# Layer 0's attention: the modulation rows summed by pairs of K-tiles over all 1024 columns, and turned into columns once per part

## The chip, the cores and the metric

The kernel runs on one core of one Trainium2 chip. The metric is the device time of one execution in microseconds (us); a lower time is better. The engines are PE (TensorE: matmuls and transposes; its weight loads are PEld), DVE (VectorE), ACT (ScalarE), POOL (GpSimd) and SP (SyncE, which issues nearly all DMA transfers). Each engine works through its own queue in order, and the engines wait for one another by semaphores.

## The reference, cut to what matters

The reference is a block of two transformer layers over 512 latent and 256 context tokens of width 1024. Each layer needs six modulation vectors of 1024 numbers (shift, scale and gate, for attention and for the FFN), each of them for two streams, latent and context:

```
s_c = silu(c);  s_cc = silu(c_ctx)
mx = s_c  @ mod_w[l] + mod_b[l]        # 1024 x 6144, latent stream
mc = s_cc @ mod_w[l] + mod_b[l]        # the same weights, context stream
shx1, scx1, gx1, shx2, scx2, gx2 = split(mx, 6)
hx = rms(x, norm_mix_w) * (1 + scx1) + shx1
x  = x + gx1 * attention(hx, hc)
x  = x + gx2 * swiglu(rms(x, norm_ffn_w) * (1 + scx2) + shx2)
```

Parts 0 and 1 (shift and scale of the attention) are needed at once. Part 2 is the gate of the attention's output. Parts 3 and 4 are the FFN's shift and scale. These three parts are what the change is about. All arithmetic is float32, with the large matmuls split into a high and a low float32r half.

## The kernel before

**The modulation in chunks.** `mod_steps` (L168 to L192) computes 256 columns of one part. It loads the weights in two pieces of four K-tiles (two DMAs of 512 KB with rows of 256 numbers, L177). Eight matmuls (L182) then multiply each K-tile (128 rows) by `s_pad`, a 128x32 tile whose first two columns are the latent and the context vector. The array is used as four column groups: K-tiles 0 to 3 go to the four groups, K-tiles 4 to 7 are added to the same groups. The PSUM tile `mod` then holds, in partitions 32j and 32j+1, the sums of K-tiles j and j+4. ACT copies it to the SBUF tile `modr` (L185). At the generator's `yield` the caller may do other work. The second half "turns" the rows: for each of the two blocks of 128 columns one matmul (L191) has `modr` as its stationary operand and the two selector columns `sel2` as its moving one, which sums the four groups and gives one column for each stream, `modcol`. `add_mod` (L273) has DVE add the bias (L276, into `modc`) and, for the two scale parts, form `aff` (L280). The tiles `mod` and `modcol` both lie in PSUM bank `acc0`.

**Where the chunks stand in the attention.** Layer 0's attention is a list of 24 steps: four head blocks b, each over six token tiles. Every step makes the scores of one tile (L578), the softmax (maximum on DVE, L587 or L591; exponential on ACT, L592; scaling on POOL, L604), the transposes of the probabilities (`ppt`, L612, copied back by ACT at even and DVE at odd key tiles, L617 and L615) and the products with the values (`av`, L623). Between these stand the input projections of the next head block (`inps`, L465, in bank `acc0`) and the transposes of its queries and keys (`qpt` L535 and `kpt` L543, copied by ACT, L537 and L544). `mod_run` (L1273) starts a chunk at the end of those steps that `RUNS` names (L1285), twelve in all: three parts by four chunks. `mod_ends` (L1279) does the second half of a started chunk in the following step, behind the first score matmul (L1306).

**What sets the order.** From step 5 of the list on, PE's instructions keep the order in which they are written (`manual_schedule`, L1294). Before that, PE's order, and everywhere the order of the other engines, comes from a planner that simulates a timeline.

**Shared room.** The weights of the chunks and the input projection's weights (`wir`, loaded at L491 for a later head block) share the two SBUF slots of the tag `raw`. So a `wir` load waits until the matmuls of the chunk before it have read their slot; ACT then makes the high half (`wihi`, L498), and DVE or POOL the low one (`wilo`, L499). Small transposes take the PSUM banks `tr0` and `tr1` in turn: `tr_tile` (L102) flips a counter at each call. `ppt` names its bank itself (`tr0` for even key tiles, `tr1` for odd).

**The gates.** `gate_mem` (L285) transposes one stream of a gate part into 8 rows of 128 (`gps`, L288), DVE copies them (`grow`, L290) and a DMA writes them to memory (L292). `gate_row` (L294) reads them back as 1024 numbers broadcast to all partitions (`g`, L300), in time for the residual (L471).

Of the kernel before, what the change touches and what calls it, by code (L numbers as in the profile page):

```python
# [11 lines left out]
F32 = mybir.dt.float32  # L12
# [7 lines left out]
P = 128  # L20
D = 1024
KT = D // P
# [15 lines left out]
MODS0 = (0, 2, 2, 0)  # L38
LAM_INIT = 0.8 - 0.6 * math.exp(-0.3)

C_ID, C_S2, C_ONE, C_S4 = 0, 128, 130, 258
C_N = C_S4 + 12


def swap_pairs(ap):
# [12 lines left out]
def dram_rows(ap, n=P):  # L58

    return AP(ap.tensor, ap.offset, [[0, n]] + [list(d) for d in ap.ap])  # L60
# [3 lines left out]
def backbone(es: ExitStack, tc: tile.TileContext, x, c, ctx, c_ctx, mod_w, mod_b, norm_mix_w, norm_ffn_w,  # L64
# [3 lines left out]
    nc = tc.nc  # L68
# [33 lines left out]
    def tr_tile(name, shape, dt=F32, one=None):  # L102
        if one is None:
            one = turn["tr"] = 1 - turn["tr"]
        return p_1.tile(shape, dt, name=name, tag=f"tr{one}")
# [16 lines left out]
    start = Pool("start")  # L122
# [45 lines left out]
    def mod_steps(l, part, n, new_tile, pool, bank, wide=None, room=("modr", 1)):  # L168
# [22 lines left out]
            nc.tensor.matmul(pc2[:, b, :], r[:, b * P:(b + 1) * P], sel2, start=True, stop=True)  # L191
        add_mod(l, part, k0, k1, pc2, 2)  # L192

    def mod_chunk(*args, **kw):
        for _ in mod_steps(*args, **kw):
            pass
# [85 lines left out]

    gmem = {}

    def gate_mem(l, part, i, bank=None):  # L285

        ps = tr_tile("gps", [KT, P]) if bank is None else p_1.tile([KT, P], F32, name="gps", tag=bank)
        nc.tensor.transpose(ps, modc[l][:, part, :, i], ident)  # L288
        row = small.tile([KT, P], F32, name="grow", tag="grow", bufs=2)
        nc.vector.tensor_copy(row, ps)  # L290
        mem = gmem[l, part, i] = dram.tile([KT, P], F32, name="gmem", tag=f"gmem{l}{part}{i}")
        nc.sync.dma_start(mem, row)  # L292

    def gate_row(l, part, i, pool):  # L294

        if (l, part, i) not in gmem:
            gate_mem(l, part, i)
        g = pool.tile([P, D], F32, name=f"g{i}", tag=f"g{i}")
        with tc.issue_after(turn["load"].ins):
            nc.sync.dma_start(g, dram_rows(gmem[l, part, i].rearrange("k p -> (k p)")))  # L300
        return g


# [909 lines left out]
            project(begun[t], t, ws, 0, 384, range(k, k + 2))  # L1213
    manual.__exit__(None, None, None)

    mods = [(0, part, n) for part in (2, 3, 4) for n in range(4)]
    tabs = {}
    tables0(0, tabs, wp.pool)

# [31 lines left out]
        turned0()  # L1251
    o_t = [keep.tile([P, KT, P], F32, name=f"o{t}", tag="xo", bufs=6) for t in range(NT)]
    steps = [(b, t) for b in range(4) for t in (CTX_FIRST if b < 3 else range(NT))]
    attend, mod_runs = {}, []

    def scores0(i):
        if i not in attend:
# [14 lines left out]

    def mod_run(n):  # L1273
        for _ in range(n):
            if mods:
                mod_runs.append(mod_steps(*mods.pop(0), raw_tile, at.pool, "acc0"))
                next(mod_runs[-1])

    def mod_ends():  # L1279
        while mod_runs:  # L1280
            for _ in mod_runs.pop(0):
                pass

    QUARTS = ((((2, 2),) * 6), ((2, 2),) * 6, ((2, 2), (2, 2), (4, 2), (2, 4), (2, 2), (0, 0)))
# [5 lines left out]
    if True:  # L1290
        for i, (b, t) in enumerate(steps):
            j = i % NT
            if i == 5:
                manual = tc.manual_schedule(engines={mybir.EngineType.PE})  # L1294
                manual.__enter__()
            if j == 0 and b < 3:
                ws += units
                proj = in_proj0(b + 1, ws, tabs, wp.pool, (even if b % 2 else odd).pool, due)
                nxt = next(proj)
            if j == 4 and b < 2:  # L1300
                units = weights0(b + 2, wp.pool, (nc.gpsimd, nc.vector))
                next(units)
            if b < 3:
                n = QUARTS[b][j]
                scores0(i)
                mod_ends()  # L1306
                transposes0(i - 1)
                scores0(i)
                projected(n[0])
                transposes0(i - 1)  # L1310
                scores0(i)
                scores0(i)
                if j == 0 and b == 1:
                    tables0(1, tabs, wp.pool)
                projected(n[1])
                transposes0(i - 1)
                values0(i - 1)
                if j == 4 and b < 2:
                    ws = [next(units) for _ in range(2)]
                while b == 2 and j == NT - 1 and due:  # L1320
                    due.pop(0)()
                mod_run(RUNS[b][j])
                if b == 1 and j == NT - 1:
                    mod_ends()
                    for k in range(2):
                        gate_mem(0, 2, k)
                if j == NT - 1:
                    state = nxt
                continue
            if t == 0:  # L1330
                scores0(i)
                mod_ends()
                transposes0(i - 1)
                scores0(i)
                transposes0(i - 1)
                scores0(i)
                scores0(i)
                transposes0(i - 1)
                values0(i - 1)
                mod_run(1)  # L1340
                mod_ends()
                wp.close()
                even.close()
                wp = Pool("w0", "right")
                opa = Pool("opa", "right")
                xs = [None] * NT
                units = out_units0(wp.pool)
                ws = [next(units)]
                oproj = OutProj(0, ws, o_t, xs)
                oproj.gates(opa.pool)  # L1350
                continue
            scores0(i)
            if t < 3:
                with behind("exp"):
                    ws += islice(units, 1)
                transposes0(i - 1)
                scores0(i)
                with behind("exp"):
                    ws += islice(units, t - 1)
                transposes0(i - 1)  # L1360
                scores0(i)
                with behind("exp"):
                    ws += islice(units, 1)
                scores0(i)
            else:
                scores0(i)
                with behind("exp"):
                    ws += units
                oproj.sums(t - 3, 0, opa.pool, nc.vector, range(1))
                transposes0(i - 1)  # L1370
                scores0(i)
                transposes0(i - 1)
                scores0(i)
                if t == 4:
                    room = [z[:, 0] for z in ctx_room([P, 1, KT, P], F32, "nroom")]
                oproj.sums(t - 3, 0, opa.pool, nc.vector, range(1, 2))
            transposes0(i - 1)
            values0(i - 1)
            if t > 3:
                for _ in norm_steps(t - 4, xs[t - 4], 0, 1, None, room=room):  # L1380
                    pass
            if t == NT - 1:
                open_ctx()
            oproj.operand(t - 1)
# [105 lines left out]
            if gates:  # L1490
                gate_mem(*gates.pop(0), "acc1")

    gates = [(0, 5, 0), (0, 5, 1), (1, 2, 0)]

    def next_raw0(name):
        return ring.pool.tile([P, 4, P], F32, name="wr", tag="wr", bufs=6)
# [112 lines left out]
    if True:  # L1609
# [32 lines left out]
            nc.sync.dma_start(subln, dram_rows(od_subln[0]))  # L1642
            nc.gpsimd.tensor_scalar(subln, subln, 1.0 - LAM_INIT, 1.0, ALU.mult, ALU.mult)
        xs0, xs1 = xs, [None] * NTX
        gate_mem(1, 5, 0)
        o_t = [keep.tile([P, D], F32, name=f"o{t}", tag="xo", bufs=6) for t in range(NTX)]
        xs = xs1
        attend = {}
# [228 lines left out]
def _constants():  # L1877
# [3 lines left out]
    k[:, C_S2] = p % 32 == 0  # L1881
    k[:, C_S2 + 1] = p % 32 == 1
    k[:, C_ONE:C_ONE + P] = 1.0
    k[:, C_S4:C_S4 + 4] = p[:, None] == 32 * np.arange(4)
    t = np.arange(SEQ)
    nf = HD // 4
    inv = np.float32(THETA) ** (-np.arange(nf, dtype=np.float32) / np.float32(nf))
# [43 lines left out]
```

## Time and profile before

| | |
|---|---|
| time of the kernel, median of 3 runs | 1696.72 us (1691.99, 1696.72, 1697.31) |
| the profiled execution | span 1695.6 us from its first to its last instruction; of what lies around the span no figure is recorded |
| instructions | 28585 |
| PE busy | 1631.5 us, 96% of the span |
| DVE, ACT, POOL busy | 1146.7 us (68%), 937.0 us (55%), 696.4 us (41%) |
| mean granted TensorE clock | 0.992 of 2.4 GHz |
| layer 0's attention | from about 60 to 390 us of the span; the twelve chunks at 90.6 to 311 us |

In the timeline, a row gives the start in us, the time from the start of the first to the end of the last instruction in it, the engine, the line, the operation and the tiles, and how many instructions it merges; in brackets stands the idle time of the engine just before, and what ended it. A float32 matmul is recorded as two instructions. Matmuls overlap in the pipeline, so the step from one row's start to the next one's tells what a row costs better than its length does.

### The profile page before, as it was taken

What the parts mean: (1) busy time and instruction counts of PE and PEld (TensorE: products, weight loads), DVE (VectorE), ACT (ScalarE), POOL (GpSimd) and SP (SyncE); (2) the same over time, 40 slices, a digit from 0 to 9 for tenths busy, and PEclk for the clock granted to TensorE, in tenths of its full rate; (3) what the DMA queues carried; (4) which work ended last, traced back from release to release, by engine and by line L of the source; (5) the groups of instructions that cost most, each with busy time, mean ns of one, the idle gap of its engine ahead of it and who ended that gap; (6) DMA issues with size and microseconds to landing.
All of it is one profiled execution on the core that took longest, in us unless ns stands there. A gap on an engine that the chain in (4) does not pass through costs nothing. (4 is left out here: it accounts for less than half of the span.)

```text
span 1695.6 us, 28585 instructions
## 1 busy us (share of the span) xinstructions
PE 1631.5 (96%) x10390; PEld 1468.6 (87%) x10390; DVE 1146.7 (68%) x2014; ACT 937.0 (55%) x2011; POOL 696.4 (41%) x867
## 2 busy tenths in 40 slices
PE   6999999899999999999999989999999999999998
PEld 3977787677999999998777889999988899999887
DVE  3765656754799887767767656666666598887434
ACT  5565555745456665545554456666666555555320
POOL 2665554321346554412413366666664242221000
PEclk8999999999999999999999999999999999999999
DMA  9222221411455555439966311111112433331431
GB/s 319 69 71 74 70 70 50 164 60 38 129 167 172 164 159 162 134 108 347 296 184 189 99 43 38 48 42 44 50 45 97 125 93 102 111 101 57 137 99 62
DMA packets 218108, 194.64 MB, mean 115 GB/s; under 512 B 20016, under 2 KB 202864, under 8 KB 217968
## 3 DMA queue, kind: packets, MB, share of 16 engines
q1 hardware_dynamic: 217616, 192.62, 36.8%
q8 instruction: 81, 1.33, 0.3%
q14 instruction: 59, 0.48, 0.1%
q10 hardware_dynamic: 352, 0.21, 0.0%
HBM read 179.92 MB, written 12.87 MB: 114 GB/s over the span
## 5 line engine op out<-in xcount | busy, mean ns | idle before, releaser
L901 ACT CAST wbh<-wr 128x512 fp32r<-128x512 f32 x170 | 104.9, 621 | 130.2 <-PE p L933 73.4
L933 PE MATMUL p<-hT,wbh 128*128 128x256 f32 (+1 forms) x752 | 154.5, 299 | 0.0
L465 PE MATMUL inps<-wih,hT 128*128 128x384 f32 x512 | 144.2, 344 | 7.3 <-ACT qkv L677 7.3
L911 POOL TENSOR_TENSOR wbl<-wr,wbh 128x512 fp32r<-128x512 f32 x43 | 60.0, 1396 | 173.6 <-ACT wbh L901 173.6
L933 PEld LDWEIGHTS p<-hT,wbh 128*128 128x128 f32 x752 | 121.9, 191 | 0.2
L911 DVE TENSOR_TENSOR wbl<-wr,wbh 128x512 fp32r<-128x512 f32 x127 | 107.7, 858 | 21.0 <-ACT wbh L901 16.8
L933 PE MATMUL p<-hT,wbl 128*128 128x256 f32 (+1 forms) x376 | 111.9, 298 | 0.0
L933 PE MATMUL p<-t,wbh 128*128 128x384 f32 (+1 forms) x480 | 111.3, 318 | 0.0
L604 POOL TENSOR_SCALAR Pt<-Pt,rc 128x256 f32<-128x256 f32 (+3 forms) x96 | 74.6, 788 | 89.3 <-DVE rc L601 83.1
L231 POOL TENSOR_TENSOR modp<-modp 128x512 f32<-128x512 f32 x40 | 57.4, 1436 | 114.3 <-ACT modp L230 114.3
L465 PEld LDWEIGHTS inps<-wih,hT 128*128 128x128 f32 x512 | 93.3, 188 | 10.6 <-ACT qkv L677 9.7
L933 PE MATMUL p<-hTt,wbh 128*128 128x256 f32 (+1 forms) x480 | 101.0, 302 | 0.0
L887 POOL TENSOR_TENSOR wr<-wr 128x512 f32<-128x512 f32 x40 | 61.6, 1540 | 89.8 <-DVE ws L892 85.8
L933 PE MATMUL p<-b,wbh 128*128 128x384 f32 x368 | 93.8, 336 | 0.2 <-DVE c L961 0.2
L901 ACT CAST wbh<-ws 128x512 fp32r<-128x512 f32 x120 | 69.4, 579 | 43.1 <-PE p L933 29.0
L224 DVE SCALAR_TENSOR_TENSOR ma<-modw,cols,ma 128x256 f32<-128x256 f32 x140 | 89.2, 637 | 2.3
L592 ACT ACTIVATE Pt<-sc,nm 128x256 f32<-128x256 f32 (+3 forms) x96 | 67.6, 707 | 35.3 <-DVE nm L588 16.9
L465 PE MATMUL inps<-wil,hT 128*128 128x384 f32 x256 | 86.0, 336 | 0.0
L933 PEld LDWEIGHTS p<-t,wbh 128*128 128x128 f32 x480 | 82.9, 189 | 0.0
L911 DVE TENSOR_TENSOR wbl<-ws,wbh 128x512 fp32r<-128x512 f32 x120 | 81.7, 681 | 1.7 <-ACT wbh L901 1.6
L933 PEld LDWEIGHTS p<-hTt,wbh 128*128 128x128 f32 x480 | 78.3, 191 | 3.1 <-ACT modp L230 1.6
L230 ACT ACTIVATE modp<-modw,cols 128x256 f32<-128x256 f32 x160 | 68.4, 500 | 18.0 <-POOL ma L236 10.1
(355 smaller groups left out, 5217.9 us busy)
## 6 DMA issues: line engine op xcount, KB each, us to landing
modw<-in_mod_w_dram SPq DMA_DIRECT2D x96, 512.0 KB, 5.2
wr<-in_ffn_w_in_dram SPq DMA_DIRECT2D x176, 256.0 KB, 2.9
wdr<-in_ffn_w_out_dram SPq DMA_DIRECT2D x66, 512.0 KB, 3.7
wir<-in_od_w_in_dram SPq DMA_DIRECT2D x96, 128.0 KB, 2.3
hidm<-hid SPq DMA_DIRECT2D x44, 192.0 KB, 1.9
hr<-hidm SPq DMA_DIRECT2D x22, 192.0 KB, 3.5
x<-in_x_dram SPq DMA_DIRECT2D x8, 512.0 KB, 3.5
wir<-in_ev_w_in_dram SPq DMA_DIRECT2D x16, 256.0 KB, 3.5
```

Source lines behind the costliest of these rows:

```text
L224: nc.vector.scalar_tensor_tensor(acc, w[:, k], scale[k], acc, ALU.mult, ALU.add)
L230: nc.scalar.activation(pr[:, k], w[:, k], AF.Copy, scale=scale[k])
L231: nc.gpsimd.tensor_add(pr[:, 0:2], pr[:, 0:2], pr[:, 2:4])
L465: nc.tensor.matmul(ps, hs[j][:, k, :], ws[k // 2][z][:, k % 2, c0:c1], start=(k, j, z) == (0, 0, 0), stop=(k, j, z) == (KT - 1, 1, 0))
L592: turn["exp"] = nc.scalar.activation(p[:, :n], s, AF.Exp, bias=nm[:, c1], accum_out=sm[:, c1])
L604: nc.gpsimd.tensor_scalar(p[:, :n], p[:, :n], rc[:, hh:hh + 1], 1.0, ALU.mult, ALU.mult)
L887: nc.gpsimd.tensor_sub(w, raw[f, "G1"], w)
L901: nc.scalar.copy(hi, w)
L911: (nc.gpsimd if name == "G2" else nc.vector).tensor_sub(lo, raw[need[n]], f32(hi))
L933: nc.tensor.matmul(ps, w[:, k, :], H[b][h][:, k, :], start=first and k == 0 and q == 0, stop=final and k == 3 and q == 2, skip_group_check ...
```

## The change

It concerns parts 2, 3 and 4 of layer 0, and the way in which gates are written to memory.

A new generator `mod_part` computes a whole part of 1024 columns in four steps. Each step takes two K-tiles, loads them with two DMAs of 512 KB (each row now 1024 numbers), and runs eight matmuls: for each K-tile, the four blocks of 256 columns go to the four column groups, and the second K-tile is added to the first in PSUM. In the first step of a part ACT copies the PSUM tile to `r`; in the other three DVE adds it to `r`. After the fourth step `r` holds the sums of all K-tiles. Two matmuls with eight selector columns (`C_S8`) then turn all 1024 columns, and `add_mod` runs once for the whole part. `mod_run` still does one step at a time and in the same places, and `mod_ends` now finishes only a part whose fourth step is done.

`gate_mem` turns both streams with one transpose of 16 columns, one DVE copy and one DMA. The rows lie in memory as tile, stream, 128 numbers, so that `gate_row` reads eight pieces of 128 numbers for each partition. `gate_mem` for part 2 now takes one `tr` bank where it took two.

```diff
-C_ID, C_S2, C_ONE, C_S4 = 0, 128, 130, 258
-C_N = C_S4 + 12
+C_ID, C_S2, C_ONE, C_S4, C_S8 = 0, 128, 146, 290, 298
+C_N = C_S8 + 20
...
+    def mod_part(l, part, new_tile, pool, bank):
+
+        r = pool.tile([P, 256], F32, name="modr", tag="modr", bufs=2)
+        for k in range(0, KT, 2):
+            ps = p_1.tile([P, 256], F32, name="mod", tag=bank)
+            for a in range(2):
+                w = new_tile([P, D], "modw")
+                nc.sync.dma_start(w, mod_w[l, (k + a) * P:(k + a + 1) * P, part * D:(part + 1) * D])
+                for n in range(4):
+                    nc.tensor.matmul(ps[32 * n:32 * n + 32, :], s_pad[:, k + a, :], w[:, n * 256:(n + 1) * 256],
+                                     start=a == 0, stop=a == 1, tile_position=(0, 32 * n))
+            if k:
+                nc.vector.tensor_add(r, r, ps)
+            else:
+                nc.scalar.copy(r, ps)
+            yield k == KT - 2
+        pc = p_1.tile([P, KT, 2], F32, name="modcol", tag=bank)
+        for b in range(2):
+            nc.tensor.matmul(pc[:, b::2, :], r[:, b * P:(b + 1) * P], cst[:, C_S8:C_S8 + 8], start=True, stop=True)
+        add_mod(l, part, 0, KT, pc, 2)
...
-    def gate_mem(l, part, i, bank=None):
+    def gate_mem(l, part, streams, bank=None):
...
+        shape = [KT * streams, P]
+        ps = tr_tile("gps", shape) if bank is None else p_1.tile(shape, F32, name="gps", tag=bank)
+        cs = modc[l][:, part].rearrange("p k i -> p (k i)") if streams == 2 else modc[l][:, part, :, 0]
+        nc.tensor.transpose(ps, cs, ident)
+        row = small.tile([2 * KT, P], F32, name="grow", tag="grow", bufs=1)[:KT * streams]
         nc.vector.tensor_copy(row, ps)
+        mem = dram.tile([KT, streams, P], F32, name="gmem", tag=f"gmem{l}{part}")
+        gmem.update({(l, part, i): mem[:, i, :] for i in range(streams)})
+        nc.sync.dma_start(mem.rearrange("k i p -> (k i) p"), row)
...
-            nc.sync.dma_start(g, dram_rows(gmem[l, part, i].rearrange("k p -> (k p)")))
+            nc.sync.dma_start(g.rearrange("p (k c) -> p k c", c=P), dram_rows(gmem[l, part, i]))
...
-    mods = [(0, part, n) for part in (2, 3, 4) for n in range(4)]
+    mods = [2, 3, 4]
...
     def mod_run(n):
         for _ in range(n):
-            if mods:
-                mod_runs.append(mod_steps(*mods.pop(0), raw_tile, at.pool, "acc0"))
-                next(mod_runs[-1])
+            if not mod_runs:
+                mod_runs.append(mod_part(0, mods.pop(0), raw_tile, at.pool, "acc0"))
+            if next(mod_runs[0]):
+                mod_done.append(mod_runs.pop(0))
 
     def mod_ends():
-        while mod_runs:
-            for _ in mod_runs.pop(0):
+        while mod_done:
+            for _ in mod_done.pop(0):
                 pass
...
                 if b == 1 and j == NT - 1:
-                    mod_ends()
-                    for k in range(2):
-                        gate_mem(0, 2, k)
+                    gate_mem(0, 2, 2)
...
                 mod_run(1)
-                mod_ends()
                 wp.close()
...
             scores0(i)
+            mod_ends()
...
-    gates = [(0, 5, 0), (0, 5, 1), (1, 2, 0)]
+    gates = [(0, 5, 2), (1, 2, 1)]
```

## Rows read from the trace of the kernel before

**Rows 1.** Busy us of each engine in a stretch (x instructions); clock, DMA share.
```profile
60.00:334.00 274.00, 254.17 (x1886) 206.62 (x1885) 174.87 (x414) 166.73 (x427) 148.36 (x230) 0.99 0.26 82
```
**Rows 2.** The turning matmuls by tile; ns min/median/max, first and last start, forms.
```profile
L191 PE MATMUL modcol<-cst,modr x80: 165/251/374, 13.3 to 312.0; 128*128 128x2 f32 x80
```
**Rows 3.** PE's timeline at the sixth of the twelve chunks.
```profile
190.23 0.56 PE L191 MATMUL modcol<-cst,modr 128*128 128x2 f32 x4
190.65 1.07 PE L612 MATMUL ppt<-cst,Pt 128*128 128x128 f32 x8
```
**Rows 4.** PE's timeline where a turn is waited for, and the gates' transposes.
```profile
95.64 0.44 PE L465 MATMUL inps<-wihi,hT 128*128 128x384 f32 x1 [1.01 <-DVE modc L276]
...
109.61 0.44 PE L465 MATMUL inps<-wihi,hT 128*128 128x384 f32 x1 [0.65 <-DVE modc L276]
...
220.24 0.61 PE L191 MATMUL modcol<-cst,modr 128*128 128x2 f32 x4 [0.49 <-ACT modr L185]
220.71 0.38 PE L288 MATMUL gps<-cst,modc 128*8 128x128 f32 x2
...
311.62 0.61 PE L191 MATMUL modcol<-cst,modr 128*128 128x2 f32 x4 [0.55 <-ACT modr L185]
```
**Rows 5.** SP's timeline, loads for a later head block (one of four places).
```profile
219.38 2.42 SPq L491 DMA_DIRECT2D wir<-in_ev_w_in_dram  x5
```
**Rows 6.** ACT's timeline behind those two loads.
```profile
193.60 0.83 ACT L498 CAST wihi<-wir 128x768 fp32r<-128x768 f32 x1 [0.90 <-DMA wir<-in_ev_w_in_dram]
...
223.83 0.83 ACT L498 CAST wihi<-wir 128x768 fp32r<-128x768 f32 x1 [1.83 <-DMA wir<-in_ev_w_in_dram]
...
225.95 0.59 ACT L537 CAST qt<-qpt 128x512 fp32r<-128x512 f32 x1
```
**Rows 7.** PE's timeline behind such loads.
```profile
157.00 1.22 PE L612 MATMUL ppt<-cst,Pt 128*128 128x128 f32 x6 [1.25 <-POOL Pt L604]
...
198.29 1.12 PE L612 MATMUL ppt<-cst,Pt 128*128 128x128 f32 x4 [2.92 <-ACT qt L537]
...
225.23 0.63 PE L612 MATMUL ppt<-cst,Pt 128*128 128x128 f32 x4
226.60 0.66 PE L612 MATMUL ppt<-cst,Pt 128*128 128x128 f32 x4 [0.73 <-ACT qt L537]
```
**Rows 8.** PE's timeline, waits of the transposes for the copied keys.
```profile
267.28 1.09 PE L612 MATMUL ppt<-cst,Pt 128*128 128x128 f32 x8 [0.69 <-ACT kT L544]
...
295.06 1.09 PE L612 MATMUL ppt<-cst,Pt 128*128 128x128 f32 x8 [0.46 <-ACT kT L544]
```
**Rows 9.** PE's timeline in the last head block, a wait for the exponential.
```profile
317.79 0.96 PE L578 MATMUL sc<-kT,qt 128*128 128x256 f32 x4 [1.59 <-ACT Pt L592]
```
**Rows 10.** DVE's timeline just after a chunk's matmuls: the second, sixth and twelfth chunk.
```profile
107.67 0.83 DVE L587 TENSOR_REDUCE mx<-sc 128x1 f32<-128x640 f32 x1 [1.32 <-PE sc L580]
...
190.43 0.82 DVE L587 TENSOR_REDUCE mx<-sc 128x1 f32<-128x640 f32 x1
...
312.26 0.16 DVE L276 TENSOR_TENSOR modc<-modcol,bcol 128x4 f32<-128x4 f32 x1 [3.58 <-PE modcol L191]
```
**Rows 11.** The tiles g and mod: a DVE product by form; who waited for mod.
```profile
L1101 DVE TENSOR_TENSOR dps<-dps,g x2: 433/433/433, 1689.4 to 1692.1; 128x256 f32<-128x256 f32 x2
...
  ACT modr L185: 9.2, 12
```
**Rows 12.** The tile g: its loads, its first users, and its landing.
```profile
L471 DVE TENSOR_TENSOR rtmp<-ops,g x11: 684/692/693, 341.5 to 1319.0; 128x512 f32<-128x512 f32 x11
...
L300 SPq DMA_DIRECT2D g<-gmem x6: 327/422/452, 311.6 to 1569.4; - x6
...
DMA to landing us min/median/max: 7.6/8.0/8.4
```
**Rows 13.** Busy times of a stretch where layer 0's FFN output begins (last: GB/s).
```profile
762.00:790.00 28.00, 28.00 (x128) 23.44 (x127) 19.65 (x33) 12.88 (x22) 5.13 (x5) 1.00 1.01 335
```
**Rows 14.** Busy times and granted clock around the longest of PE's waits.
```profile
195.00:204.00 9.00, 6.08 (x34) 5.17 (x32) 5.34 (x9) 3.87 (x10) 3.85 (x6) 0.81 0.38 117
```

More of the change, by code (lines that the diff above doesn't have):

```diff
@@ L283, in backbone @@
     gmem = {}
-    def gate_mem(l, part, i, bank=None):
-        ps = tr_tile("gps", [KT, P]) if bank is None else p_1.tile([KT, P], F32, name="gps", tag=bank)
-        nc.tensor.transpose(ps, modc[l][:, part, :, i], ident)
-        row = small.tile([KT, P], F32, name="grow", tag="grow", bufs=2)
+    def gate_mem(l, part, streams, bank=None):
[4 more added lines that the diff above has]
+        row = small.tile([2 * KT, P], F32, name="grow", tag="grow", bufs=1)[:KT * streams]
         nc.vector.tensor_copy(row, ps)
-        mem = gmem[l, part, i] = dram.tile([KT, P], F32, name="gmem", tag=f"gmem{l}{part}{i}")
-        nc.sync.dma_start(mem, row)
+        mem = dram.tile([KT, streams, P], F32, name="gmem", tag=f"gmem{l}{part}")
+        gmem.update({(l, part, i): mem[:, i, :] for i in range(streams)})
+        nc.sync.dma_start(mem.rearrange("k i p -> (k i) p"), row)
     def gate_row(l, part, i, pool):
         if (l, part, i) not in gmem:
-            gate_mem(l, part, i)
+            gate_mem(l, part, 1)
         g = pool.tile([P, D], F32, name=f"g{i}", tag=f"g{i}")
         with tc.issue_after(turn["load"].ins):
-            nc.sync.dma_start(g, dram_rows(gmem[l, part, i].rearrange("k p -> (k p)")))
+            nc.sync.dma_start(g.rearrange("p (k c) -> p k c", c=P), dram_rows(gmem[l, part, i]))
         return g
@@ L1253, in backbone @@
     steps = [(b, t) for b in range(4) for t in (CTX_FIRST if b < 3 else range(NT))]
-    attend, mod_runs = {}, []
+    attend, mod_runs, mod_done = {}, [], []
     def scores0(i):
@@ L1644, in backbone @@
         xs0, xs1 = xs, [None] * NTX
-        gate_mem(1, 5, 0)
+        gate_mem(1, 5, 1)
         o_t = [keep.tile([P, D], F32, name=f"o{t}", tag="xo", bufs=6) for t in range(NTX)]
@@ L1883, in _constants @@
     k[:, C_ONE:C_ONE + P] = 1.0
-    k[:, C_S4:C_S4 + 4] = p[:, None] == 32 * np.arange(4)
+    k[:, C_S4:C_S4 + 8] = p[:, None] == 32 * (np.arange(8) % 4) + 16 * (np.arange(8) // 4)
+    k[:, C_S8:C_S8 + 8] = p[:, None] == 32 * (np.arange(8) // 2) + np.arange(8) % 2
     t = np.arange(SEQ)
```

## The prediction

> **What bounds the kernel now.** I read the page first, then the busy times by stretch, PE's timeline over the attention of layer 0, and what PE waits for there. In the stretch that holds all twelve chunks PE is busy 254.17 of 274 us, DVE 174.87, ACT 166.73 and POOL 148.36, and the DMA engines have a share of 0.26 [rows 1]. So PE sets the pace, with short waits for ACT, DVE and POOL between its work. PE's waits there name no transfer directly. From the third chunk on PE's order is fixed by hand, so an instruction that PE doesn't have to do moves everything behind it forward, unless the next thing PE waits for isn't moved too. That "unless" is the question of this case.
>
> **The turns that go.** A turn is four recorded instructions [rows 2] (80 for the 20 chunks of the kernel, eight of which stand before the attention and stay). From a turn's start to the next row's start PE needs 190.65 - 190.23 = 0.42 us [rows 3]. Twelve turns become three, each with 8 moving columns in place of 2; the old median of 0.251 us for 2 columns is nearly all fixed cost, so I price a new turn like an old one (below by 0; above, if each of its two matmuls took as long as the gates' 128-column transposes, two of which take 0.38 us, no more than 0.42 again). Nine turns less are 9 x 0.42 = 3.8 us.
>
> **The waits around them.** After the first two chunks the next projection waits for `modc`, since rows, columns and projection share one bank: 1.01 and 0.65 us. The turn of the seventh chunk stands straight behind its matmuls, because the old code ends it before the gates, and waits 0.49 us for ACT's copy; so does the twelfth, 0.55 us [rows 4]. The first three waits go with their turns: 2.15 us. The twelfth's turn stays but moves behind the next step's first scores, so its 0.55 us goes too. The gates of part 2 take one transpose where two took 0.38 us: 0.1 us less. The sum so far is 3.8 + 2.15 + 0.55 + 0.1 = 6.6 us.
>
> **What is swallowed.** Four chunks (the second, third, sixth and seventh) are followed by loads of the next head block's weights. They need the slots that the chunk's matmuls have just read, so SP issues them right behind these matmuls [rows 5] (one of the four). ACT stands in its queue at the cast of that load, 0.90 us in one place and 1.83 us in the other, with exponentials and the copy of the transposed queries behind it [rows 6], and PE then waits for what is behind it: 2.92 us at 198.29 for the query copy, 0.73 us at 226.60 for the same, 1.25 us at 157.00 for POOL, which has a low half of these weights in its queue as well [rows 7]. These ends hang on the chunk's matmuls plus a transfer, not on the turn. So what the change saves between such a chunk and such a wait only makes the wait longer: 0.42 us each at the third and sixth chunk, 0.42 + 0.49 + 0.1 = 1.0 us at the seventh. After the second chunk there is the same kind of load, but only shorter waits; I take half of 0.42 + 0.65, that is 0.5 us. Together 0.4 + 0.4 + 1.0 + 0.5 = 2.3 us are lost, and 4.3 us left. Below, nothing is swallowed (0); above, all of the second's (2.9 us).
>
> **The banks of the small transposes.** One `gate_mem` call in place of two flips the turn of `tr0` and `tr1` once instead of twice. From there on queries go to `tr0`, keys to `tr1`, the reverse of before. The probabilities' transposes begin with `tr0`. At 225.23 four of them run before the wait for the query copy and four behind it [rows 7]; now all eight stand behind it: 0.66 us is the length of the four, about 0.5 us is what they add. Where the wait is for the key copy, 0.69 and 0.46 us [rows 8], four transposes can now go ahead, which gives back up to the same 0.5 us each; queries that are copied late elsewhere cost it again. I take 0.3 us for all of it: 4.0 us left (between -0.7 and +1.5 us).
>
> **The last head block.** There scores wait for the exponential, 1.59 us at 317.79 [rows 9], and the moved turn of the last part adds its 0.42 us before it is clear what ends the next wait. I take off 0.5 us: 3.5 us left (0 to 1.4 us, the ninth to twelfth chunk's 0.42 us each less what carries).
>
> **What DVE takes over.** Nine additions of 128x256 with one operand in PSUM. The trace has a product of that size out of PSUM at 433 ns [rows 11]: 9 x 0.43 = 3.9 us of DVE, while nine of its twelve bias additions (0.16 us each) go. ACT loses nine copies. Just after the chunk's matmuls DVE sits idle at eight of the nine places: the first has 1.32 us before its maximum, the last 3.58 us; only at the sixth chunk is its queue full [rows 10]. The bank is wanted only after two score blocks and eight transposes, about 2.4 us later. So I cost the additions at nothing on PE's path. Bounds: below nothing too, a gain of at most the nine copies that leave ACT, which I leave out since ACT waits there anyway; above, see the second rival.
>
> **What else moves.** The weights come in as 24 loads of 512 KB as before, in the same places and slots, with longer rows; no wait of PE depends on them. In SP's queue one store of gates stands where two did, ahead of the last load of the seventh chunk's five and one [rows 5]; that frees SP earlier, and the cast that binds is the first one's. The gates come back in pieces of 128 numbers: a load landed in 8.0 us, and its first user in layer 0 comes at 341.5 us, after an issue at 311.6 us [rows 12]. So even two loads one behind the other and twice as slow (32 us) would be late by only 2 us, and I take nothing. The gates of part 5 are read where the FFN's output begins and the DMA engines are full, 1.01 at 335 GB/s [rows 13]: if short pieces made these two loads (1 MB, 3.1 us at that rate) twice as dear, later weights would land 3.1 us later. PE is busy 28.00 of 28 us there, fed by loads made ahead, so I take nothing of that either.
>
> **The sum.** 6.6 - 2.3 - 0.3 - 0.5 = 3.5 us. Against the profiled span of 1695.6 us that is 1692.1 us; the record of this execution has no time beside its span, and the median of the runs stands 1.1 us above the span, so I put 1.1 us around it: 1693.2 us, which is also the median less 3.5 us. Everything behind the attention is PE's own work in an order fixed by hand, and moves with it.
>
> **Rivals.** (a) All of it arrives: the planner, which sees ACT free of nine copies, brings the query copies and exponentials forward, and nothing is swallowed. Then 6.6 us: 1690.1 us; with shorter waits for ACT, some 1689. For it: ACT stood 9.2 us in twelve waits for the chunks' matmuls [rows 11], and that goes. Against it: the waits of rows 7 end with a transfer.
>
> (b) Slower: DVE takes over ACT's place in the queue. If the planner puts the addition ahead of work that is ready (the query chain or a maximum), DVE stands as ACT did, 9.2 / 12 = 0.77 us each, plus 0.43 us for the addition. If all of that reached PE through the maxima and the copied probabilities, it would be 9 x 1.2 = 10.8 us, and 1693.2 + 10.8 = 1704.0 us. It decides from 3.5 / 9 = 0.39 us that each addition costs PE. For it: the full queue at the sixth chunk; against it: the idle DVE at the eight others [rows 10].
>
> (c) The clock. The wait of 2.92 us at 198.29 is followed by a lower clock: from 195 to 204 us the mean granted clock is 0.81, that is, part of it at 1.2 instead of 2.4 GHz, and 0.19 x 9 = 1.7 us are lost [rows 7, 14]. If the wait at 226.60 grows from 0.73 us by the 1.0 us swallowed and the 0.5 us of transposes that no longer run ahead of it, it is 2.2 us long, and a second stretch of low clock may follow: 1693.2 + 1.7 = 1694.9 us. The Trainium skill says the like (TensorE: Matmul & The Clock Gate, What's actually happening): the slow clock is the default, and only activity lifts it, so a longer idle PE pays twice. By that rule the longer wait costs these 1.7 us; the trace agrees for the long wait, with 0.81, and for the short one no row shows it yet.
>
> (d) The change does less than it says. Up to step 5 PE's own order is the planner's, and the two largest waits (1.01 and 0.65 us) lie there. If it fills the freed places otherwise, these two and their turns (2 x 0.42) give nothing: 2.5 us less 0.5 us counted as swallowed, so 1693.2 + 2.0 = 1695.2 us.
>
> **How the numbers follow.** The forecast has 0.45, (a) 0.22, (b) 0.09, (c) 0.12, (d) 0.12. The bounds of the unknown terms around the forecast (2.3 swallowed at its ends 0 and 2.9; the banks -0.7 to +1.5; the last block 0 to 1.4) add to some -3.5 to +2.7 us: 1689.7 to 1695.9 us. The range reaches to just past (a) and to most of (d) and (c) with the spread of the runs: 1687.5 to 1699.5 us. A measurement of this kernel can tell about 0.3%, 5.1 us: faster is below 1691.6 us, slower above 1701.8 us. Faster: (a) nearly whole, 0.20, and 0.18 of the forecast's lower part: 0.38. Slower: (b) where most of its price is paid, 0.07, and 0.02 for a plan that goes wrong elsewhere: 0.09. The same: the rest, 0.53.
>
> **What would show it.** Right: 44 recorded instructions on the turning line (11 turns of four, 32 of them before the attention) instead of 80; no wait for `modc` by the projections after the first two chunks; DVE additions of about 0.43 us that follow the chunk's matmuls at once, with the projection behind them not waiting; the waits behind the sixth and seventh chunk's weight loads longer by 0.4 and by 1.0 to 1.5 us; attention's end earlier by 3 to 4 us and the same distance kept up to the end. Wrong: waits of PE for the new addition or for maxima behind it (b), a new stretch of low clock near 227 us (c), waits at the same places as short as before although PE comes earlier (a), or a difference that first arises far behind the attention, which none of these steps has.

## The result, and the profile after

The changed kernel takes 1703.32 us (median of 5 runs, 1701.96 to 1707.23); the kernel before took 1696.21 us beside it (1691.99 to 1697.31). The ratio is 1.0050 with a 95% interval of 1.0039 to 1.0061, so it is slower by 7 us in the medians, 6.6 to 10.3 us by the interval. Forecast were 1693.2 us and, at most, 1699.5 us. The profiled execution spans 1700.2 us against 1695.6 us; it is the fastest of the five. One run of the kernel `gates_only` below took 1796.22 us at a granted clock of 0.85; its ratio is of the other seven runs.

What the change promises is there. In the rows of the tile `modr` (line, engine, operation, count, ns min/median/max, first and last start), 32 records of the old turn stand ahead of the attention, 12 of the new one in it, 256 ns each, where [rows 2] had 80; nine additions stand on DVE, 0.42 us each:

```profile
L191 PE MATMUL modcol<-cst,modr x32: 167/252/376, 13.4 to 46.1; 128*128 128x2 f32 x32
L212 PE MATMUL modcol<-cst,modr x12: 170/256/257, 168.1 to 312.1; 128*128 128x8 f32 x12
L206 DVE TENSOR_TENSOR modr<-modr,mod x9: 406/421/422, 100.1 to 311.2; 128x256 f32<-128x256 f32 x9
L208 ACT COPY modr<-mod x3: 366/372/372, 89.8 to 274.5; 128x256 f32<-128x256 f32 x3
```

The waits for `modc` and `modr` [rows 4] have no counterpart. The same stretches as in [rows 1] and [rows 14], with the same columns: in the first, PE is busy about as long with 48 instructions fewer, and 37 of these are the ones that the change takes away (36 of the turns, one gate transpose); the granted clock is 0.98, it was 0.99. The second has the same 0.81 as before:

```profile
60.00:334.00 274.00, 253.47 (x1838) 203.30 (x1837) 174.94 (x405) 163.75 (x416) 145.34 (x227) 0.98 0.25 81
...
195.00:204.00 9.00, 6.87 (x38) 5.96 (x38) 4.50 (x10) 4.99 (x13) 3.03 (x4) 0.81 0.40 120
```

To see where the time went, take the same instruction in both traces and subtract the starts. PE's timeline after, at waits that exist in both kernels or are new:

```profile
73.45 0.53 PE L559 MATMUL qpt<-identr,qd 128*128 128x128 f32 x4 [0.59 <-ACT qt L561]
...
110.87 1.44 PE L602 MATMUL sc<-kT,qt 128*128 128x256 f32 x4 [2.69 <-ACT Pt L616]
...
158.81 1.22 PE L636 MATMUL ppt<-cst,Pt 128*128 128x128 f32 x6 [0.64 <-POOL Pt L628]
...
198.75 1.12 PE L636 MATMUL ppt<-cst,Pt 128*128 128x128 f32 x4 [2.13 <-ACT qt L561]
...
210.11 0.33 PE L636 MATMUL ppt<-cst,Pt 128*128 128x128 f32 x1 [1.62 <-POOL Pt L628]
210.88 0.76 PE L636 MATMUL ppt<-cst,Pt 128*128 128x128 f32 x5 [0.45 <-POOL Pt L628]
...
227.88 1.09 PE L636 MATMUL ppt<-cst,Pt 128*128 128x128 f32 x8 [0.80 <-ACT qt L561]
...
316.29 0.97 PE L602 MATMUL sc<-kT,qt 128*128 128x256 f32 x4 [0.69 <-ACT Pt L616]
...
323.00 0.33 PE L636 MATMUL ppt<-cst,Pt 128*128 128x128 f32 x1 [0.69 <-POOL Pt L628]
...
339.00 0.51 PE L832 MATMUL ops<-wol,hT 128*128 128x512 f32 x1 [0.21 <-DVE wol L799]
```

and the first and the last of them before:

```profile
76.06 0.54 PE L535 MATMUL qpt<-identr,qd 128*128 128x128 f32 x4 [0.64 <-ACT qt L537]
...
339.56 0.51 PE L808 MATMUL ops<-wol,hT 128*128 128x512 f32 x1 [0.25 <-DVE wol L775]
```

At the first of these instructions the changed kernel is 2.6 us ahead (73.45 against 76.06); the start differs from kernel to kernel (it stands there at 73.45 to 77.60 us in those that leave the first steps to the planner), and I don't count on it. The wait that stood at 157.00 us [rows 7] comes at 158.81 us: 4.4 us lost in between. The one at 317.79 us [rows 9] comes at 316.29 us: 3.3 us won in between, although 2.07 us of new waits for POOL lie there. Of these 3.3 us, 0.9 are lost again at once: from there to the first wait of the output product are 22.71 us (316.29 to 339.00), and they were 21.77 (317.79 to 339.56); a wait for POOL at 323.00 us lies in between. Behind the attention the product with `g` begins 0.6 us earlier than in [rows 12], the FFN's output 3.6 us later (851.3 us before), and the last products 4.5 us later than in [rows 11]:

```profile
L495 DVE TENSOR_TENSOR dps<-dps,g x19: 692/699/700, 854.9 to 1692.4; 128x512 f32<-128x512 f32 x19
L495 DVE TENSOR_TENSOR rtmp<-ops,g x11: 684/692/692, 340.9 to 1323.3; 128x512 f32<-128x512 f32 x11
...
L1125 DVE TENSOR_TENSOR dps<-dps,g x2: 433/433/433, 1693.9 to 1696.5; 128x256 f32<-128x256 f32 x2
```

So there are three separate things: a gain in the middle of the attention (3.3 us, of which 2.4 are left at its end), a loss in its first steps, and a loss behind the attention, in a stretch where the change has no instruction. In the stretch from 460 to 740 us PE is busy 280 of 280 us in both kernels, yet fits in 13 instructions fewer (columns as in [rows 1]); before and after:

```profile
460.00:740.00 280.00, 280.00 (x1648) 275.28 (x1647) 236.13 (x396) 159.47 (x326) 134.59 (x108) 1.00 0.52 156
```
```profile
460.00:740.00 280.00, 280.00 (x1635) 275.24 (x1634) 231.89 (x391) 158.98 (x325) 134.22 (x108) 1.00 0.51 155
```

13 x 280 / 1648 = 2.2 us, at a granted clock of 1.00 in both.

### The profile page after: what moved, and what is told of

Its sections match the earlier page's. It is cut to its first block, busy times and chain, and to the rows that moved or that the text cites. A ratio compares the mean times of both kernels' runs of the same rounds, so it can differ in the third digit from the quotient of the medians.

```text
span 1700.2 us, 28499 instructions
## 1 busy us (share of the span) xinstructions
PE 1636.7 (96%) x10352; PEld 1470.2 (86%) x10352; DVE 1146.3 (67%) x2009; ACT 934.4 (55%) x2002; POOL 697.1 (41%) x867
## 5 line engine op out<-in xcount | busy, mean ns | idle before, releaser
L935 POOL TENSOR_TENSOR wbl<-wr,wbh 128x512 fp32r<-128x512 f32 x43 | 59.4, 1382 | 176.1 <-ACT wbh L925 176.1
L957 PEld LDWEIGHTS p<-t,wbh 128*128 128x128 f32 x480 | 82.9, 189 | 0.0
L935 DVE TENSOR_TENSOR wbl<-ws,wbh 128x512 fp32r<-128x512 f32 x120 | 81.7, 681 | 1.7 <-ACT wbh L925 1.6
```

Source lines behind the costliest of these rows:

```text
L935: (nc.gpsimd if name == "G2" else nc.vector).tensor_sub(lo, raw[need[n]], f32(hi))
L957: nc.tensor.matmul(ps, w[:, k, :], H[b][h][:, k, :], start=first and k == 0 and q == 0, stop=final and k == 3 and q == 2, skip_group_check ...
```

## Experiments

Each was timed in 5 to 12 runs beside the kernel before; ratios are to it, and 0.001 is 1.7 us. The theories at first: P, the planner's new order of the first steps; D, DVE's additions; B, the flipped banks of the small transposes; A, the places of tiles in memory. For A one must know that the changed kernel's constant tile has 318 columns where it had 270, so that what follows it starts 192 B later in every partition, and that the gates' row has one buffer instead of two, which brings what follows that 512 B back (192 - 512 = -320 B). Most tiles move so; those allotted from the other end don't.

**First set: order, gates, sums.** PE's order by hand from the first step of the attention on, in both kernels:

```diff
-            if i == 5:
+            if i == 0:
                 manual = tc.manual_schedule(engines={mybir.EngineType.PE})
```

> The kernel before, with PE's order fixed by hand from the first step of layer 0's attention instead of the sixth. It is the partner of the next run, and says what the planner's own order of PE in those five steps is worth. If the planner (theory P: the loss comes from orders that the planner chose anew) does well there in the kernel before, this is slower by 0 to 4 us: 1696 to 1700 us. If the planner's order doesn't matter, it is within 1 us of the kernel before.

Measured: 1702.89 us, 1.0046 (1.0033 to 1.0058), above the range that either theory gave. The planner's order of the first steps is worth some 8 us in the kernel before.

> The changed kernel with PE's order fixed by hand from the first step of layer 0's attention. Theory P (the planner pulled the projection ahead after the second chunk, so that scores stand without cover near 110 us): the wait of 2.7 us for the exponential near 110 us and the low clock behind it go, and this is 2 to 4 us faster than its partner, and 4 to 7 us faster than the changed kernel (1697 to 1699 us). Theory D (the additions on DVE cost by themselves, the second rival of the prediction): still 5 to 8 us slower than its partner, with PE waits behind the additions.

Measured: 1709.93 us, 1.0086 (1.007 to 1.0101), 7 us above its partner. So the planner's order alone isn't the loss.

The change cut in two: the gates with the 318 constants, and the sums without them (274 constants, old gates).

```diff
-C_N = C_S4 + 12
+C_N = C_S8 + 20
...
-    def gate_mem(l, part, i, bank=None):
+    def gate_mem(l, part, streams, bank=None):
```

> The kernel before with the new way of writing and reading the gates alone, and with the changed kernel's larger constants, which move every tile behind them by 192 bytes; the sums stay as before. Theory B (the flipped banks of the small transposes cost): 0.3 to 2 us slower, with longer waits for the query copies from 222 us on. Theory A (the moved addresses make layer 0's FFN slower, where the changed kernel lost 2.4 us in small steps): 2.4 us slower in the stretch from 460 to 750 us. Theories P and D: within 1.5 us of the kernel before.

Measured: 1700.8 us, 1.0031 (1.002 to 1.0041).

```diff
-C_ID, C_S2, C_ONE, C_S4, C_S8 = 0, 128, 146, 290, 298
-C_N = C_S8 + 20
+C_ID, C_S2, C_ONE, C_S4, C_S8 = 0, 128, 130, 258, 266
+C_N = C_S8 + 8
...
-    gates = [(0, 5, 2), (1, 2, 1)]
+    gates = [(0, 5, 0), (0, 5, 1), (1, 2, 0)]
```

> The changed kernel with the gates written and read as before, one buffer for the row sums, and constants 16 bytes larger than before instead of 192. Theories P and D: all of the loss of 7 us is here (1702 to 1704 us). Theory B: 1 to 2 us faster than the changed kernel. Theory A: the slow drift of 2.4 us in layer 0's FFN is gone, 1701 us.

Measured: 1698.7 us, 1.0027 (1.0017 to 1.0037), less than any theory gave. Two halves, both slower; and from 460 to 740 us the kernel with the 318 constants has 1634 PE instructions, the one with 274 has 1643, before_hand 1647. That count follows the number of constants, not the gates or the sums.

**Second set: only the place.**

```diff
-C_N = C_S4 + 12
+C_N = C_S4 + 60
...
-        row = small.tile([KT, P], F32, name="grow", tag="grow", bufs=2)
+        if (l, part) not in grow:
+            grow[l, part] = small.tile([32 + KT, P], F32, name="grow", tag="grow", bufs=1)
+        row = grow[l, part][32 * i:32 * i + KT]
```

> The kernel before with the same instructions and nothing of the change, only moved: the constants get 48 unused columns (318 as in the changed kernel, 192 B more per partition), and the two rows of a gate share one tile, which frees the 512 B that this needs. Theory A (moved tiles make PE's matmuls slower): 3 to 5 us slower than before, 1698 to 1700 us, and the drift of 2.4 us between 460 and 740 us as in the changed kernel. Theory P and theory D (the loss comes from the order of the early steps and from DVE's additions): 1694 to 1696.5 us, and no drift.

Measured: 1701.31 us, 1.0035 (1.0025 to 1.0045). Without any of the change's work, 5.9 us (4.2 to 7.6) are lost by moving tiles. The FFN's matmuls show how. Rows of the tile `b`, the moving operand of 445 of them, before and in the moved kernel:

```profile
L933 PE MATMUL p<-b,wbh x296: 331/335/339, 459.9 to 737.2; 128*128 128x384 f32 x148
```
```profile
460.00:740.00 280.00, 280.00 (x1634) 275.32 (x1633) 235.56 (x392) 158.35 (x323) 134.32 (x108) 1.00 0.52 156
...
L935 PE MATMUL p<-b,wbh x297: 336/337/343, 459.7 to 733.0; 128*128 128x384 f32 x149
```

and of the tile `t`, which lies at the other end of the memory and did not move, before and in the moved kernel:

```profile
L933 PE MATMUL p<-t,wbh x296: 333/334/346, 464.2 to 735.1; 128*128 128x384 f32 x148
```
```profile
L935 PE MATMUL p<-t,wbh x296: 332/334/340, 466.4 to 739.7; 128*128 128x384 f32 x148
```

The stationary operand `wbh` is of the same kind in both and keeps its place in this stretch. Where the moving one has moved, the fastest matmul takes 336 ns in place of 331; where it hasn't, the median stays at 334. The step from one such matmul's start to the next one's says it more clearly, as matmuls overlap: its mean over the stretch (both halves of the weights, steps under 230 ns) is 173.5 ns for `b` before and 176.2 in the moved kernel, and for the other moved operand `hT` 173.6 and 176.1. In the changed kernel it is 176.2 for both.

The change with its constants packed to 270, and the same with the old buffers too:

```diff
+C_ID, C_S2, C_ONE, C_S4, C_S8 = 0, 128, 130, 258, 262
+C_N = C_S8 + 8
...
-        row = small.tile([2 * KT, P], F32, name="grow", tag="grow", bufs=1)[:KT * streams]
+        row = small.tile([2 * KT, P], F32, name="grow", tag="grow", bufs=2)[:KT * streams]
```

> The changed kernel with its selector columns packed into the 270 constants of the kernel before, so that what follows the constants keeps its place; the gates' row still takes one buffer where two were (tiles behind it move by 512 B), and the row sums still have two buffers. Theory A, if any move counts: still slow, 1700 to 1703 us. Theory A, if the constants' move counts: 1696 to 1699.5 us, drift near 0. Theories P and D: as the changed kernel, 1701 to 1703 us.

Measured: 1698.83 us, 1.0020 (1.0009 to 1.0031); 1648 instructions from 460 to 740 us.

> The changed kernel with constants in the old 270 columns, two buffers for the gates' row (each 512 B as before) and one for the row sums: all of the change's instructions, and tiles outside of the attention at their old places. Theory A: the drift is gone, and what is left is the planner's order of the first steps (up to 4 us lost) against the sums' gain (4 us): 1693 to 1698 us. Theories P and D: 1701 to 1703 us, as the changed kernel.

Measured: 1699.45 us, 1.0020 (1.001 to 1.0029), above the 1698 us that theory A allowed; 1647 instructions. The move by 512 B alone does nothing, and by these ratios place explains more than half of the loss, not all.

> The kernel before with the gates' part of the change alone and its constants unchanged, the gates' row in two buffers as before. Theory A: 1694 to 1696 us, the kernel before within 1 us, and no drift; the same gates with the moved constants took 1700.8 us. Theory B (the flipped banks of the small transposes): stays at 1699 to 1701 us.

Measured: 1696.89 us, 1.0003 (0.9993 to 1.0013), 1648 instructions. The gates cost nothing that these runs can tell (at most 2.2 us by the interval); the flipped banks are out as the cause of the loss.

**Third set: which moves, and the sums without the early steps.**

```diff
-C_N = C_S4 + 60
+C_N = C_S4 + 44
```

> The kernel before moved by other amounts: 32 unused columns of constants instead of 48, so that the tiles behind them move by 128 B instead of 192 and those behind the gates' row by 384 B down instead of 320. Nothing else differs from the kernel that was moved by 192 and 320 B (1701.3 us, 1.5% longer 384-column matmuls wherever the moving operand had moved). If the place within 128 B decides: matmuls as in the kernel before, no drift between 460 and 740 us, 1694 to 1697 us. If any move counts, or the distance to the tiles that stay: drift of 2 us or more, 1699 to 1702 us.

Measured: 1694.03 us, 0.9995 (0.9986 to 1.0003):

```profile
460.00:740.00 280.00, 280.00 (x1647) 275.28 (x1646) 236.82 (x396) 159.47 (x325) 134.60 (x108) 1.00 0.51 156
...
L935 PE MATMUL p<-b,wbh x297: 332/336/336, 459.7 to 737.5; 128*128 128x384 f32 x149
```

This kernel and before_moved differ in 16 unused columns and in nothing else, so it is the place that costs. Moves by multiples of 128 B (+128, -384, -512) cost at most one instruction there; +192 and -320 cost 13 or 14 instructions in 280 us, and +32 (the 274 constants of sums_only) costs 5. The step on `b` agrees: 173.1 ns here, 173.8 at +32 B.

It isn't simply the place modulo 128 B, though. In the programs' memory plans `b` and `hT` start at a multiple of 128 B before, and 64 B past one after the costly moves; but `t` starts 64 B past one in every kernel, and its step is 174.5 ns before, 173.6 in the moved kernel and 175.4 here, though it never moved. So the places of other tiles have a part in it; which do, no run tells.

> The changed kernel at the old addresses with PE's order fixed by hand from the first step of the attention on instead of from step 5; its partner is the kernel before with that order (1702.9 us, 1.0046 of before). Theory S (the sums give what the prediction's sum says, and the planner's own order of the first steps, with its low clock near 110 us, takes it back): 2.5 to 5 us faster than the partner, 1698 to 1700.5 us. Theory D (DVE's additions cost PE): not faster than the partner, 1702 to 1706 us.

Measured: 1705.97 us, 1.0068 (1.0053 to 1.0083): 3 us slower than its partner, not faster. My theory S was wrong there; its trace shows new waits for POOL's scaling near 140 and 218 us, the same kind as at 210 us after the change.

```diff
-    mods = [2, 3, 4]
+    mods = [(0, 2, n) for n in range(4)] + [3, 4]
```

> Old addresses, the gates' part of the change, part 2 in four chunks of 256 columns as before and only parts 3 and 4 by sums over pairs of K-tiles. So the first steps, where the planner orders PE, have the instructions of before. Theory S: no low clock near 110 us, and the eight later steps give their part, six turns of 0.42 us and the waits of 0.49 and 0.55 us less what is swallowed, about 2 us: 1692 to 1695 us. Theory D: 1697 to 1700 us.

Measured: 1694.69 us, 1.0001 (0.9989 to 1.0013). PE's timeline and the stretch from 70 to 160 us of this kernel:

```profile
74.00 0.53 PE L559 MATMUL qpt<-identr,qd 128*128 128x128 f32 x4 [0.64 <-ACT qt L561]
...
154.96 1.22 PE L636 MATMUL ppt<-cst,Pt 128*128 128x128 f32 x6 [1.00 <-POOL Pt L628]
...
206.09 0.33 PE L636 MATMUL ppt<-cst,Pt 128*128 128x128 f32 x1 [1.63 <-POOL Pt L628]
...
70.00:160.00 90.00, 82.74 (x606) 67.58 (x605) 58.66 (x175) 56.61 (x162) 56.45 (x96) 1.00 0.23 69
```

From the first to the second row are 80.96 us, as before (157.00 - 76.06 = 80.94); the changed kernel takes 85.36 us, and the other kernels with sums in the first steps 85.0 to 85.9 us, the moved kernels and those with the gates alone 81.7 to 82.0, and late_order below, which has the sums of sums_late, 82.9. So the sums of the first two chunks, not those of the later ones, cost 2 to 5 us there, 3.6 between the means. The wait at 206 us stays, though.

**Fourth set: POOL's order.** Before, POOL scales the probabilities and then works on the query norms; after, the other way round. POOL's timeline, before and after:

```profile
205.74 1.79 POOL L604 TENSOR_SCALAR Pt<-Pt,rc 128x640 f32<-128x640 f32 x2
207.62 0.32 POOL L159 TENSOR_SCALAR rs_q<-qss 128x5 f32<-128x5 f32 x1
208.02 1.17 POOL L160 TENSOR_TENSOR rs_q<-rs_q,neghalf 128x5 f32<-128x5 f32 x1
```
```profile
207.66 0.36 POOL L159 TENSOR_SCALAR rs_q<-qss 128x5 f32<-128x5 f32 x1 [1.11 <-DVE qss L466]
208.10 1.17 POOL L160 TENSOR_TENSOR rs_q<-rs_q,neghalf 128x5 f32<-128x5 f32 x1
209.26 1.57 POOL L628 TENSOR_SCALAR Pt<-Pt,rc 128x640 f32<-128x640 f32 x2
```

The edit queues the norms behind the scaling, at one tile or (by hand order) at two; PE's order stays:

```diff
-            y, r = rotate(raw[:, 0:320], 4, 1, t, *tabs[b // 2], wp)
+            with behind("scale") if (b, t) == (2, 2) else ExitStack():
+                y, r = rotate(raw[:, 0:320], 4, 1, t, *tabs[b // 2], wp)
```

> As the kernel with part 2 in chunks and parts 3 and 4 by sums, with one thing more: at one token tile (the fifth of the third head block's projection) POOL's two operations for the query norms are queued behind the scaling of the probabilities, as they stand in the kernel before; in every kernel with the sums they stand ahead of it, and PE waits there 1.6 and 0.45 us for the scaling. PE's order is untouched. Theory Q (the sums change the queues of POOL, DVE and ACT at one place, and PE pays 2.1 us there): both waits gone, 1 to 3 us faster than without it, 1691.5 to 1693.8 us. If the waits come from DVE's addition itself: no change, 1694.5 to 1696 us.

Measured: 1694.19 us, 0.9991 (0.998 to 1.0002), 1.7 us less than without by the ratios, which is within their intervals. The waits are not gone: the first falls from 1.63 to 0.79 us, the second stays at 0.45.

> The changed kernel with its constants packed into the old 270 columns, and POOL's order mended at the same one place. Theory Q: 1 to 3 us faster than the packed kernel's 1698.8 us, 1696 to 1697.8 us; what is left over the kernel before is the planner's order of the first steps with its low clock near 110 us. Otherwise: 1698 to 1700 us.

Measured: 1697.0 us, 1.0011 (1.0 to 1.0021); 1.5 us less, and again the intervals meet.

> The changed kernel at the old addresses with PE's order by hand from the first step (1706.0 us), and POOL's order mended at the two places where it differs from the same kernel without the change (1702.9 us): the fifth tile of the second and of the third block's projection. With it both have the same orders around the chunks. Theory Q: waits of 1.9 and 0.45 us near 140 us and 1.65 and 0.4 us near 218 us go, with the low clock behind the latter: 4 to 6 us faster, 1700 to 1702 us, and so 1 to 3 us faster than the kernel without the change, which is the sums' own gain. Otherwise: 1704 to 1707 us.

Measured: 1700.8 us, 1.0030 (1.0017 to 1.0042), against 1.0068 without the mended order: 6.4 us less, intervals apart. PE's wait and the granted clock behind it, first without and then with it:

```profile
218.01 0.39 PE L636 MATMUL ppt<-cst,Pt 128*128 128x128 f32 x1 [1.65 <-POOL Pt L628]
...
214.00:226.00 12.00, 9.96 (x68) 8.50 (x65) 6.11 (x19) 5.01 (x14) 6.25 (x10) 0.86 0.00 0
```
```profile
212.21 0.33 PE L637 MATMUL ppt<-cst,Pt 128*128 128x128 f32 x1 [0.79 <-POOL Pt L629]
...
208.00:220.00 12.00, 10.76 (x83) 8.83 (x81) 7.17 (x21) 6.48 (x19) 7.21 (x14) 1.00 0.03 11
```

Here too the first wait is halved and not gone as I expected, and the second stays (0.39 and 0.45 us): POOL's scaling now waits 1.59 us for DVE's reciprocal, which stands behind the query's products in DVE's queue. With the order mended the change comes out 2.7 us below its partner (1.0030 against 1.0046), but the intervals of these two overlap, so a gain by the sums is not shown.

## Why the prediction was wrong, step by step

Two steps failed above all. "What else moves" held nothing for the places of the tiles, and they cost 5.9 us (4.2 to 7.6). And the sum counted 2.0 us as won at the first two chunks, where 4.4 us were lost.

**The turns and their waits: right.** Nine turns are gone, the new ones cost no more than the old, and the four waits for `modc` and `modr` went.

**What is swallowed, and the banks: too cautious.** For the part behind the second chunk the prediction's terms leave 7 x 0.42 + 0.49 + 0.55 + 0.1 - 1.8 - 0.3 - 0.5 = 1.5 us. Measured, between the waits of [rows 7] and [rows 9], are 3.3 us, or 5.4 us without the new waits for POOL. The waits behind the weight loads did not grow by what was saved ahead of them (2.92 us became 2.13, 0.73 became 0.80), those for the copied keys [rows 8] are gone, and the wait for the exponential fell from 1.59 to 0.69 us. The two halves tell these apart: gates_packed, with the flipped banks alone, has lost the waits for the keys (1.15 us) and kept the 1.59 us; sums_only, without the flip, kept the first and has 0.68 us. But at the same tiles gates_packed waits 0.31 and 0.68 us for the copied queries, where before it was 0.21: the banks gave some 0.4 us there where I let them cost 0.3. Some of the 5.4 us is spread over such waits and not traced one by one. And the 0.9 us of the exponential were not kept: the last stretch of the attention takes 22.70 to 22.72 us in every kernel with the sums of parts 3 and 4, and 21.76 to 21.78 in every one without. There "the last head block" was right that something else ends the next wait. The net gain at the attention's end is 3.3 - 0.9 = 2.4 us. (The prediction's lower bound of -3.5 us takes the banks' -0.7 as a difference from the 0.3 us, its upper one of +2.7 takes their +1.5 as a cost; it shifts one end by 0.3 us.)

**The planner, rival (d): the right place, the wrong size.** I let the first two chunks' places give nothing, 2.0 us less than the forecast. They cost 4.4 us against before (3.6 us between the means of the kernels with and without sums there). In the changed kernel the planner runs a whole projection (101.30 to 105.63 us) ahead of the scores, DVE's maximum for these comes late, and PE waits 2.69 us at 110.87 us. The clock falls with it, to 1.2 of 2.4 GHz for part of the stretch:

```profile
110.00:120.00 10.00, 9.13 (x50) 6.57 (x50) 4.80 (x14) 6.45 (x17) 4.82 (x9) 0.66 0.05 20
```

0.34 x 10 = 3.4 us at most, as PE is idle for some of it. PE's new order can't be all of the 4.4 us, though. With that order fixed by hand, the same stretch (from the first wait for the copied queries to the one for POOL) takes 91.95 us in before_hand (71.53 to 163.48), 95.12 in same_hand (71.06 to 166.18) and, with POOL's order mended, 93.95 in hand_order (68.86 to 162.81). So 2 to 3 us are lost there with the old order of PE too; how the rest divides stays open. The low clock is rival (c)'s mechanism in another place; where I put it, the clock from 220 to 230 us stayed at 1.00.

**What DVE takes over: the cost at nothing failed, though not as rival (b) had it.** The additions run at once and take the 0.42 us forecast; no wait of PE names them. But removing copies from ACT and adding to DVE changed the order that the planner gives DVE, ACT and POOL around 205 us, and 2.07 us of waits stand there. I weighed only the added operation, not the queues that it re-orders. With POOL's order mended some 0.8 us of such a pair of waits goes and 1.24 us stay, which hang on DVE's reciprocal. That POOL's order costs time, hand_order shows at its two places; at the one place of the changed kernel itself the runs agree, with intervals that meet.

**What else moves: the term that was missing.** The new constants stand in the diff and in no step of my sum. They and the gates' single buffer move most tiles by +192 or -320 B, and before_moved shows that this costs 5.9 us (4.2 to 7.6) by itself. I wrote that everything behind the attention "moves with it", and that a difference that first arises there would prove me wrong; it did. Of the 4.3 us that the profile of before_moved is longer (1699.9 against 1695.6 us), 14 instructions or 2.4 us lie from 460 to 740 us.

Together: +5.9 for the places, +4.4 for the early steps, -3.3 for the middle of the attention with POOL's waits in it, +0.9 for its last stretch, is 7.9 us, against 7.1 between the medians and 6.6 to 10.3 by the interval. It mixes runs and single profiles, and leaves out the 2.6 us at the start of these, so it is no proof to the tenth. Without the places it gives 2.0 us; the packed kernel measured 3.4 (1.5 to 5.3). Its 12 runs have a mean granted clock of 0.992 against 0.995 of before, some 5 us, of which the stretch near 110 us is up to 3.4. Short stretches of low clock near 850, 985 and 1270 us come in some profiles with and without the change, and not in others; why, stays open. So does how the 3.5 us or so that places cost outside of the stretch from 460 to 740 us are spread. No version tried beats the kernel before beyond its interval; late_order comes nearest.

## What to carry to other kernels

A few columns added to a shared constant tile can cost more than the edit they serve: keep tiles that PE streams where they were (here a shift of all of them by multiples of 128 B was free), and test by padding alone. Where a planner orders the engines, an operation moved from one engine to another is priced by the queue order it yields and not by its length; compare the order of every engine, POOL's too. And a saving inside a region that is ordered by hand was kept here for the most part (2.4 us), while in the first steps, which the planner filled again, it turned into a loss.

## What the runs showed of the hardware

The rate of 384-column matmuls depends on where tiles start in SBUF. With the same stationary operand, length and a granted clock of 1.00, the mean step from one to the next on the operand `b` is 173.5 ns at the old place and 176.2 ns at 192 or 320 B off (recorded durations 331 to 339 and, in before_moved, 336 to 343 ns), and 173.1 ns when all moves are multiples of 128 B. The operand's own place modulo 128 B doesn't decide it: `t`, which stays 64 B past a multiple of 128, has steps of 173.6 to 175.7 ns as the others move.

The Trainium skill (SBUF — State Buffer, Specifications) gives lines of 16 bytes in this memory. All the moves here are multiples of 32 B, so by lines of 16 bytes nothing would change; the runs disagree, 1.0035 for one such move and 0.9995 for another. The same page's section on operand start alignment asks only for multiples of the element size, and says that this is about what is allowed, not about speed.
